# Twenty of the 31 taps of one convolution chunk, on GpSimd in a sum of their own

## The chip, the core and the metric

The kernel runs on one core of a Trainium2 chip. A core has five engines that run their own instruction streams and wait for each other by semaphores: TensorE (PE in the rows, with its weight loads as PEld), VectorE (DVE), ScalarE (ACT), GpSimd (POOL) and SyncE (SP, which here issues the DMAs). The metric is the device time of one launch in microseconds (us); less is better. A row's "ns" is a thousandth of that.

## The reference, cut to what matters

A model block with three token mixers side by side and a mixture of experts is followed by two further layers, on one sequence of 256 tokens with 1024 channels, all in float32. The change lies in the convolution mixer of the first block. It has 256 channels: a gated input `z`, a causal depthwise convolution of width 31 over the tokens, a group norm, and a swish.

```python
def conv_mixer(u, w, b, gn_g, gn_b):
    a, gt = jnp.split(u, 2, axis=-1)
    z = a * jax.nn.sigmoid(gt)
    zp = jnp.pad(z, ((0, 0), (CONV_WIDTH - 1, 0), (0, 0)))
    y = lax.conv_general_dilated(zp, w[:, None, :].astype(dt), (1,), 'VALID', ...,
                                 feature_group_count=CONV_CH) + b
    ...                     # layer norm in groups of 64 channels, then silu
```

```python
mix = jnp.concatenate([o_gla, o_conv, o_diff], axis=-1)
x = x + mix @ w_out[l]
x = x + hier_moe(...)
```

## The kernel before

Channels (or features) lie on the 128 partitions and the 256 tokens along the free dimension, so 256 convolution channels are two chunks of 128 partitions, `a = 0` and `a = 1`. Every large weight matrix arrives by DMA in pieces of 128 x 2048 float32 (`raw`), is rounded by ScalarE into `hi` (L316) and VectorE computes the rest `lo = raw - hi` (L320); TensorE multiplies with both (L340 and L342, or L356 to L358 where the tokens come out on the partitions). So each piece needs ScalarE, then VectorE, then TensorE. The rings of `hi` and `lo` have four buffers each.

`mixer1` (from L744) is the stage of the change, the first 130 us of the run. It projects the input into the three mixers' operands (`psd` buffers of PSUM, two of them in the ring, read out by VectorE or ScalarE before the next projection may write them), then works out the differential attention (`diff1`), the gated linear attention (`gla`) and the convolution; last, ScalarE takes the norms of the three results (`normed`, L822 to L827) and the output projection begins. TensorE also has small products for later (L1113, on DMA'd `araw`) that fill its gaps.

The convolution reads `zp`, the gated input with 30 zero columns ahead; its two chunks are written by L771. Per chunk, VectorE does tap 0 with the bias (L843), then 30 taps, each one `scalar_tensor_tensor` on 128 x 256 (L845): `y = zp[:, a, w:w+256] * cw[w] + y`. The chunk's group mean is a matmul on TensorE (L847), VectorE subtracts it (L848) and ScalarE squares the result (L849). `cw` holds the tap weights and is there from the start.

What sets the order: the code is handed to a list scheduler, which writes one fixed order per engine; engines then run it strictly in that order. The convolution comes late in the code, so its taps are spread over VectorE's row as filler wherever the scheduler saw room, from 31.5 us to 117 us. Each engine stops at an instruction whose semaphore isn't reached, and all that stands behind it on that engine stops too. GpSimd has no work in this stage.

Of the kernel before, what the change touches and what calls it, by code (L numbers as in the profile page):

```python
# [16 lines left out]
OP = mybir.AluOpType  # L17
# [3 lines left out]
P = 128  # L21
# [203 lines left out]
class Net:  # L225
# [514 lines left out]
    def mixer1(self, hl, T):  # L740
        nc = self.nc
# [4 lines left out]
        zp = T([P, 2, 30 + S], "zp")  # L746
# [91 lines left out]
        cw = T([P, 62], "cw")  # L838
        nc.vector.tensor_scalar(cw, self.v("conv_w", 0, 62), 0.5, None, OP.mult)
        cy, sc = T([P, 2, 256], "cy"), self.w512()  # L840
        for a in range(2):
            y = cy[:, a, :]
            nc.vector.tensor_scalar(y, zp[:, a, 0:256], cw[:, 31 * a:31 * a + 1], self.v("conv_b", a), OP.mult, OP.add)  # L843
            for w in range(1, 31):
                nc.vector.scalar_tensor_tensor(y, zp[:, a, w:w + 256], cw[:, 31 * a + w:31 * a + w + 1], y, OP.mult, OP.add)  # L845
            pm = self.ps("a")
            nc.tensor.matmul(pm[:, 0:256], self.k["blk"], y, start=True, stop=True)  # L847
            nc.vector.scalar_tensor_tensor(y, pm[:, 0:256], -1.0 / 64, y, OP.mult, OP.add)  # L848
            nc.scalar.activation(sc[:, 256 * a:256 * a + 256], y, AF.Square)  # L849
# [1217 lines left out]
```

## Time and profile before

| | |
|---|---|
| median of three runs | 1417.76 us (1417.69 to 1421.76) |
| the profiled execution | 1419.36 us |
| its span (first to last instruction) | 1417.6 us |
| TensorE busy | 1365.7 us (96%) |
| VectorE busy | 1056.5 us (75%) |
| ScalarE busy | 771.6 us (54%) |
| GpSimd busy | 0.2 us |
| granted TensorE clock, mean | 0.989 of full |

Busy times are of instructions, which on one engine overlap a little: a row's duration includes the end of an instruction, under which the next one has begun. From start to start, two neighbours on VectorE are some 0.08 us closer than the duration says. The profiled execution lies 1.76 us above its span and 1.60 us above the median of the runs.

### The profile page before, as it was taken

The page shows a single profiled execution, that of the slowest core. Times are in us where ns is not written, and L with a number is a line of the kernel's source. Part 1 is how long each engine was busy: PE and PEld are TensorE (multiplying, and loading weights), DVE is VectorE, ACT ScalarE, POOL GpSimd, SP SyncE. Part 2 cuts the span into 40 slices and gives each one's busy share as a digit, 9 for nine tenths or more (in the row PEclk, how much of TensorE's full clock was granted, in tenths as well). Part 3 has the DMA queues.
Part 4 walks back from the last instruction along what each step waited for, and adds up shares of the span by engine and source line. Part 5 has one row for each costly group of instructions (what it writes and reads, how often), then busy time and mean ns, then how long its engine had stood idle before and what let it go on. Part 6 is the DMA issues. An engine that isn't in the chain of part 4 may idle for free.

```text
span 1417.6 us, 21913 instructions
## 1 busy us (share of the span) xinstructions
PE 1365.7 (96%) x8070; PEld 1093.5 (77%) x8075; DVE 1056.5 (75%) x2424; ACT 771.6 (54%) x1486; POOL 0.2 (0%) x4
## 2 busy tenths in 40 slices
PE   7998899999999999898999999999999999999997
PEld 6756575546888888666888888888888667888886
DVE  8997646537998567766998877998587586877664
ACT  7556433325665554544755556556555554766563
POOL 0000000000000000000000000000000000000000
PEclk9999899999999999999999999999999999999999
DMA  8744568886886458622687675886487632455452
GB/s 311 285 164 161 240 264 324 338 335 240 370 310 249 166 179 305 267 94 86 238 306 294 208 261 193 331 317 230 164 306 283 233 110 99 161 198 196 143 183 71
DMA packets 51391, 326.49 MB, mean 230 GB/s; under 512 B 6209, under 2 KB 7378, under 8 KB 18898
## 3 DMA queue, kind: packets, MB, share of 16 engines
q1 hardware_dynamic: 50994, 324.86, 62.3%
q8 instruction: 64, 1.05, 0.3%
q14 instruction: 45, 0.37, 0.1%
q10 hardware_dynamic: 288, 0.20, 0.1%
HBM read 324.00 MB, written 1.05 MB: 229 GB/s over the span
## 4 chain that ended last, share of the span: by engine, by line
PE 89%; DVE 5%; ACT 3%; DMA 2%; issue 1%; SPq 0%; DVEq 0%; ACTq 0%
PE psd L340 13%; PE pse L340 12%; PE psa L340 11%; PE psd L342 7%; PE pse L342 6%; PE psa L342 6%; PE psd L356 3%; PE psd L358 3%; PE psd L357 3%; PE psd L1849 3%; PE psm L1113 2%; PE pse L1849 2%; PE psa L1905 1%; PE psd L641 1%; PE pse L1526 1%
## 5 line engine op out<-in xcount | busy, mean ns | idle before, releaser
L320 DVE TENSOR_TENSOR lo<-raw,hi 128x512 fp32r<-128x512 f32 x836 | 505.2, 627 | 166.8 <-ACT hi L316 166.3
L316 ACT ACTIVATE hi<-raw 128x1024 fp32r<-128x1024 f32 (+3 forms) x420 | 402.7, 962 | 332.3 <-PE pse L340 79.2
L340 PE MATMUL psd<-hl,hi 128*128 128x512 f32 x592 | 214.3, 403 | 9.1 <-DVE hl L681 6.7
L342 PE MATMUL psd<-hl,lo 128*128 128x256 f32 x640 | 180.5, 284 | 0.0
L340 PE MATMUL pse<-hl,hi 128*128 128x512 f32 x496 | 176.2, 397 | 0.0
L340 PE MATMUL psa<-hl,hi 128*128 128x512 f32 x464 | 164.6, 396 | 0.8 <-ACT hi L316 0.6
L342 PE MATMUL psa<-hl,lo 128*128 128x256 f32 x512 | 143.7, 281 | 0.0
L342 PE MATMUL pse<-hl,lo 128*128 128x256 f32 x512 | 143.3, 280 | 0.0
L340 PEld LDWEIGHTS psd<-hl,hi 128*128 128x128 f32 x592 | 112.0, 190 | 38.5 <-ACT hi L316 8.5
L342 PEld LDWEIGHTS psd<-hl,lo 128*128 128x128 f32 x640 | 122.1, 191 | 1.7 <-DVE lo L320 1.0
L340 PEld LDWEIGHTS pse<-hl,hi 128*128 128x128 f32 x496 | 93.2, 188 | 23.7 <-issue 2.3
L340 PEld LDWEIGHTS psa<-hl,hi 128*128 128x128 f32 x464 | 87.1, 188 | 21.2 <-ACT hi L316 0.9
L342 PEld LDWEIGHTS psa<-hl,lo 128*128 128x128 f32 x512 | 96.7, 189 | 1.7 <-issue 1.0
L342 PEld LDWEIGHTS pse<-hl,lo 128*128 128x128 f32 x512 | 96.6, 189 | 0.2
L1143 DVE SCALAR_TENSOR_TENSOR acc<-araw,cact,acc 128x512 f32<-128x512 f32 x118 | 85.0, 743 | 0.8 <-DMA araw<-wada 0.8
L356 PE MATMUL psd<-hi,hl 128*128 128x512 f32 (+3 forms) x224 | 84.6, 378 | 0.8 <-ACT hl L378 0.4
L357 PE MATMUL psd<-lo,hl 128*128 128x512 f32 (+3 forms) x224 | 83.8, 374 | 0.0
L358 PE MATMUL psd<-hi,hl 128*128 128x512 f32 (+3 forms) x224 | 83.2, 374 | 0.0
L340 PE MATMUL pse<-hT,hi 128*128 128x512 f32 x220 | 77.3, 394 | 0.0
L340 PE MATMUL psd<-hT,hi 128*128 128x512 f32 x220 | 77.2, 394 | 0.0
L342 PE MATMUL pse<-hT,lo 128*128 128x256 f32 x264 | 74.1, 281 | 0.0
L342 PE MATMUL psd<-hT,lo 128*128 128x256 f32 x264 | 74.0, 280 | 0.0
(576 smaller groups left out, 2433.8 us busy)
## 6 DMA issues: line engine op xcount, KB each, us to landing
raw<-w SPq DMA_DIRECT2D x87, 1024.0 KB, 5.0
araw<-wada SPq DMA_DIRECT2D x64, 1024.0 KB, 6.9
raw<-w SPq DMA_DIRECT2D x64, 704.0 KB, 4.1
raw<-egu SPq DMA_DIRECT2D x32, 1024.0 KB, 7.2
raw<-edn SPq DMA_DIRECT2D x16, 1024.0 KB, 6.6
raw<-w2n SPq DMA_DIRECT2D x12, 1024.0 KB, 6.6
raw<-cw SPq DMA_DIRECT2D x8, 1024.0 KB, 6.3
araw<-wadb SPq DMA_DIRECT2D x8, 1024.0 KB, 5.8
```

The source lines that it names most:

```text
L316: nc.scalar.activation(hi[:, f:g], src[:, f:g], AF.Copy)
L320: ins = nc.vector.tensor_tensor(lo[:, f:g], src[:, f:g], hi[:, f:g].bitcast(F32), OP.subtract)
L340: nc.tensor.matmul(ps[:M, :].rearrange("p (a b) -> p a b", a=2), hi[:, o:o + M], xhl[:, k0 + k, :, :], start=st, stop=False)
L342: nc.tensor.matmul(ps[:M, 0:256], lo[:, o:o + M], xhl[:, k0 + k, 0, :], start=False, stop=sp)
L356: nc.tensor.matmul(o, xh, wh, start=st, stop=False)
L357: nc.tensor.matmul(o, xh, wl, start=False, stop=False)
L358: nc.tensor.matmul(o, xl, wh, start=False, stop=sp)
L641: nc.tensor.matmul(ps[:, 0:258], raw[:, o:o + P], self.xg[:, k, :], start=(k == 0), stop=(k == NC - 1))
L1113: self.together(4, lambda j: self.nc.tensor.matmul(self.ada_acc[32 * j:32 * j + 32, :n], lhsT, rhs[:, n * j:n * j + n], start=start, stop= ...
L1143: nc.vector.scalar_tensor_tensor(acc[:, w], raw[:, w], self.cact[:, c, 0:1], acc[:, w], OP.mult, OP.add)
L1526: self.halves(lambda g: nc.tensor.matmul(po[t][64 * g:64 * g + 64, 256 * rp:256 * rp + 256], vn[:, kt, P * (1 + b) + 64 * g:P * (1 + b) + ...
L1849: self.net.halves(lambda h: nc.tensor.matmul(out[p(h)], lhsT[:, p(h)], rhs(h), start=start, stop=stop, tile_position=(0, 64 * h)))
```

## The change

For chunk `a = 0`, taps 1 to 10 stay on VectorE and taps 11 to 30 go to GpSimd, which adds them up in a tile of its own, `cyp`. Tap 11 is one `tensor_scalar` there; each of the 19 others is two instructions: a `tensor_scalar` into `ctp` (one buffer) and a `tensor_tensor` that adds it to `cyp`. At the end VectorE adds `cyp` to its own sum (L857 of the changed kernel). Chunk `a = 1` keeps all its taps on VectorE. Lines after L845 move down by up to 12: VectorE's taps are L848 now, and the subtraction of the mean is L860.

```diff
         for a in range(2):
             y = cy[:, a, :]
             nc.vector.tensor_scalar(y, zp[:, a, 0:256], cw[:, 31 * a:31 * a + 1], self.v("conv_b", a), OP.mult, OP.add)
+
             for w in range(1, 31):
-                nc.vector.scalar_tensor_tensor(y, zp[:, a, w:w + 256], cw[:, 31 * a + w:31 * a + w + 1], y, OP.mult, OP.add)
+                z, c = zp[:, a, w:w + 256], cw[:, 31 * a + w:31 * a + w + 1]
+                if a or w < 11:
+                    nc.vector.scalar_tensor_tensor(y, z, c, y, OP.mult, OP.add)
+                elif w == 11:
+                    yp = T([P, 256], "cyp")
+                    nc.gpsimd.tensor_scalar(yp, z, c, None, OP.mult)
+                else:
+                    tp = T([P, 256], "ctp")
+                    nc.gpsimd.tensor_scalar(tp, z, c, None, OP.mult)
+                    nc.gpsimd.tensor_tensor(yp, yp, tp, OP.add)
+            if a == 0:
+                nc.vector.tensor_tensor(y, y, yp, OP.add)
```

GpSimd's row of the changed kernel, from the end of its start-up; 39 instructions in all, each of which waits for the one ahead of it, since `ctp` and `cyp` pass between them. The first waits for `zp` (L771), the ISA row ahead of it for nothing.

```order
L2074 UNCONDITIONAL_BRANCH
L851 ISA
L851 TENSOR_SCALAR cyp_1148<-zp_202,cw_1133 128x256
L854 TENSOR_SCALAR ctp_1150<-zp_202,cw_1133 128x256
L855 TENSOR_TENSOR cyp_1148<-cyp_1148,ctp_1150 128x256
L854 TENSOR_SCALAR ctp_1153<-zp_202,cw_1133 128x256
L855 TENSOR_TENSOR cyp_1148<-cyp_1148,ctp_1153 128x256
```

Before, that row went from its start-up straight to the branch of the expert stage.

VectorE, in the projections of the differential attention: `lo` is half a weight piece, L810 and L812 read the two `psd` buffers of one projection out. Before:

```order
L320 TENSOR_TENSOR lo_679<-raw_676,hi_678 128x512 x2
L845 SCALAR_TENSOR_TENSOR cy_1135<-zp_202,cw_1133,cy_1135 128x256 x2
L810 TENSOR_REDUCE dss_554<-w_103_630 128x8
L812 TENSOR_SCALAR dqk_629<-psd_555,r_22_198 128x512
L810 TENSOR_REDUCE dss_554<-w_104_634 128x8
```

and now:

```order
L320 TENSOR_TENSOR lo_679<-raw_676,hi_678 128x512 x2
L857 TENSOR_TENSOR cy_1135<-cy_1135,cyp_1148 128x256
L848 SCALAR_TENSOR_TENSOR cy_1135<-zp_202,cw_1133,cy_1135 128x256
L810 TENSOR_REDUCE dss_554<-w_103_630 128x8
L812 TENSOR_SCALAR dqk_629<-psd_555,r_22_198 128x512
```

VectorE's row is the same ahead of this place. One tap has given way to the sum with GpSimd's result, and that row waits for GpSimd's last instruction.

VectorE at the end of the stage, where L1017 (now L1029) reads the last attention product out, L848 (now L860) is the convolution's mean, and `lo` belongs to the output projection. Before:

```order
L1017 TENSOR_SCALAR dqk_861<-pse_1005,subg_857 128x256
L848 SCALAR_TENSOR_TENSOR cy_1135<-psa_1168,cy_1135 128x256
L845 SCALAR_TENSOR_TENSOR cy_1135<-zp_202,cw_1133,cy_1135 128x256
L1157 TENSOR_TENSOR mod_365<-psm_1297,vec 128x16
L845 SCALAR_TENSOR_TENSOR cy_1135<-zp_202,cw_1133,cy_1135 128x256
L1161 SCALAR_TENSOR_TENSOR gs_367<-mod_365,vec 128x8
L320 TENSOR_TENSOR lo_1340<-raw_1337,hi_1339 128x512
L845 SCALAR_TENSOR_TENSOR cy_1135<-zp_202,cw_1133,cy_1135 128x256
L320 TENSOR_TENSOR lo_1345<-raw_1337,hi_1344 128x512 x2
L848 SCALAR_TENSOR_TENSOR cy_1135<-psa_1203,cy_1135 128x256
```

and now:

```order
L1173 SCALAR_TENSOR_TENSOR gs_367<-mod_365,vec 128x8
L1029 TENSOR_SCALAR dqk_861<-pse_1005,subg_857 128x256
L860 SCALAR_TENSOR_TENSOR cy_1135<-psa_1208,cy_1135 128x256
L860 SCALAR_TENSOR_TENSOR cy_1135<-psa_1243,cy_1135 128x256
L827 TENSOR_TENSOR go_1113<-go_1113,w_259_1250 128x512
```

Three taps and three `lo` have left the stretch between the two rows of the mean; the taps are done earlier in VectorE's row, and the `lo` of the output projection too, five of them in the places of taps that GpSimd has taken and three a little later. From the output projection on, all engines' rows are as before.

## Rows read from the trace of the kernel before

**Rows 1.** The page: busy us, share of the span and instructions of each engine.

```profile
PE 1365.7 (96%) x8070; PEld 1093.5 (77%) x8075; DVE 1056.5 (75%) x2424; ACT 771.6 (54%) x1486; POOL 0.2 (0%) x4
```

**Rows 2.** Stretches of `mixer1`: its length, busy us (and instructions) of each engine.

```profile
core 0: us, PE busy (x) PEld busy (x) DVE busy (x) ACT busy (x) POOL busy (x), PEclk, DMA share, GB/s
24.30:51.85 27.55, 26.86 (x154) 23.39 (x152) 27.21 (x80) 18.49 (x32) 0.00 (x0) 1.00 0.75 276
51.85:78.90 27.05, 26.73 (x122) 19.60 (x121) 26.63 (x67) 12.39 (x16) 0.00 (x0) 1.00 0.68 264
78.90:114.90 36.00, 33.34 (x204) 19.21 (x201) 32.97 (x85) 18.16 (x60) 0.00 (x0) 1.00 0.48 175
114.90:119.30 4.40, 3.49 (x21) 1.47 (x22) 4.40 (x12) 0.86 (x3) 0.00 (x0) 1.00 0.00 0
```

**Rows 3.** Three of these stretches, line L845 alone: VectorE's taps.

```profile
24.30:51.85 27.55, 6.60 (x15) 1.00 0.75 276
51.85:78.90 27.05, 12.23 (x27) 1.00 0.68 264
78.90:114.90 36.00, 6.45 (x15) 1.00 0.48 175
```

**Rows 4.** VectorE's groups from 24.3 to 51.85 us: busy us, mean ns | idle before.

```profile
L320 DVE TENSOR_TENSOR lo<-raw,hi 128x512 fp32r<-128x512 f32 x22 | 14.5, 684 | 0.1
L845 DVE SCALAR_TENSOR_TENSOR cy<-zp,cw,cy 128x256 f32<-128x256 f32 x15 | 6.6, 478 | 0.0
L752 DVE SCALAR_TENSOR_TENSOR sog<-psd,w 128x256 f32<-128x256 f32 x2 | 0.8, 424 | 0.2 <-ACT w L368 0.2
L752 DVE SCALAR_TENSOR_TENSOR gqk<-psd,w 128x256 f32<-128x256 f32 x2 | 0.8, 422 | 0.1
L760 DVE TENSOR_SCALAR gv<-psd,r 128x272 f32<-128x272 f32 x1 | 0.5, 501 | 0.0
L896 DVE TENSOR_TENSOR gzk<-gqk,gqk 128x256 f32<-128x256 f32 x1 | 0.4, 419 | 0.0
L1088 DVE COPY cact<-cact 128x256 f32<-128x256 f32 x1 | 0.3, 283 | 0.0
```

**Rows 5.** VectorE in order of time: start us, us; `zp`'s first chunk, and 51.85 us.

```profile
23.90 0.41 DVE L771 SCALAR_TENSOR_TENSOR zp<-w,nrs 128x256 f32<-128x256 f32 x1
...
51.85 0.88 DVE L845 SCALAR_TENSOR_TENSOR cy<-zp,cw,cy 128x256 f32<-128x256 f32 x2
52.65 0.68 DVE L810 TENSOR_REDUCE dss<-w 128x8 f32<-128x512 f32 x1
53.24 0.74 DVE L812 TENSOR_SCALAR dqk<-psd,r 128x512 f32<-128x512 f32 x1
```

**Rows 6.** TensorE in order of time, behind those; in brackets the idle time ahead.

```profile
52.75 1.06 PE L1113 MATMUL psm<-araw,cact 128*32 128x512 f32 x8
54.13 0.47 PE L356 MATMUL psd<-hi,hl 128*128 128x512 f32 x1 [0.32 <-DVE dqk L812]
```

**Rows 7.** ScalarE in order of time, at the end of the stage.

```profile
114.04 0.38 ACT L1016 ACTIVATE w<-pse 128x256 f32<-128x256 f32 x1 [0.46 <-PE pse L1015]
115.37 0.42 ACT L849 ACTIVATE w<-cy 128x256 f32<-128x256 f32 x1 [0.94 <-DVE cy L848]
118.86 0.42 ACT L849 ACTIVATE w<-cy 128x256 f32<-128x256 f32 x1 [3.07 <-DVE cy L848]
119.25 0.69 ACT L490 ACTIVATE w<-psa,eps 128x512 f32<-128x512 f32 x1
```

**Rows 8.** Single groups of 0 to 140 us that bound GpSimd's price.

```profile
L2059 POOL MEMSET const-float32-0.0<- 128x1 f32 x1 | 0.1, 100 | 0.2 <-issue 0.2
L433 DVE MEMSET k_ghead<- 32x1 f32 x4 | 0.2, 59 | 0.1
L490 ACT ACTIVATE cy<-cy,vec 128x256 f32<-128x256 f32 x2 | 1.1, 596 | 0.0
L919 DVE COPY_PREDICATED gSA<-k_gmask,psa 128x512 f32<-128x512 uint8 x7 | 6.2, 883 | 0.2 <-PE psa L918 0.2
```

## The prediction, made before the changed kernel had run

> **What bounds the kernel now.** I read the page's first line, then the stretches of the stage, then single rows in order of time where an engine waits. The whole run is TensorE's: 96% busy, with VectorE at 75% and GpSimd at nothing [rows 1]. That makes GpSimd look free and VectorE worth relieving. But a share over 1417.6 us says nothing on 20 taps that lie in the first 120 us, so the stage has to be read in pieces [rows 2].
>
> From 24.3 us, where the first chunk of `zp` is done (23.90 + 0.41, rows 5), to 51.85 us TensorE is busy 26.86 of 27.55 us and VectorE 27.21: both are full, and neither has slack. From 51.85 to 78.9 us the same holds (26.73 and 26.63 of 27.05). From 78.9 to 114.9 us TensorE has 36.00 - 33.34 = 2.66 us of idle time, VectorE 3.03. Then, from 114.9 to 119.3 us, VectorE is busy without a break and ScalarE does 0.86 us of work: this is the tail, in which ScalarE waits 3.07 us for the mean of the second chunk [rows 7] while VectorE does three last taps and three `lo`. VectorE decides there.
>
> One more place is tight: at 51.85 us. VectorE does two taps, then L810 and L812, which read `psd` out; TensorE had filled the time with L1113 and starts its next projection at 54.13 us, after 0.32 us of waiting for L812 [rows 5, 6]. So what delays VectorE's row ahead of that L812 delays TensorE by the same amount but for nothing, and behind it TensorE has 27 us of work with 0.3 us of idle time, in which a delay can't be won back.
>
> **What the change takes away.** Twenty taps leave VectorE. A tap's row says 478 ns [rows 4]; from start to start it is 0.40 us (the two at 51.85 end where L810 starts, 0.80 us later, rows 5). That is 20 x 0.40 = 8.0 us of VectorE's work, and the new sum L857 takes the place of one more of those starts, at the 419 ns of the nearest two-input row (L896, rows 4), less than a tap. But of 8 us only what stood on the path counts, stretch by stretch:
>
> - up to 51.85 us: VectorE's row is the same as before, 15 taps included [rows 3]. Nothing is gained.
> - 51.85 to 78.9 us: 27 taps become 19, and five `lo` of the output projection move in. 8 x 0.40 = 3.2 us go, 5 x 0.60 = 3.0 come. TensorE bounds this stretch. Nothing is gained.
> - 78.9 to 114.9 us: 15 taps and one `lo` become six taps and three `lo`, so 9 x 0.40 - 2 x 0.60 = 2.4 us less. It can shorten the stretch by no more than TensorE's idle 2.66 us. That idle time has other causes too (a late `araw`, hand-overs between engines), so I take 1 us, with 0 and 2.7 as ends.
> - the tail: three taps and three `lo` are gone from between the two rows of the mean, so ScalarE's second L849 follows its first at once. Gain 3.1 us [rows 7].
>
> Together **4.1 us of gain**, between 3.1 and 5.8. What comes next on the path is ScalarE's chain of norms, which starts with L490 at 119.25 us and is unchanged.
>
> **What the change adds: 39 instructions on GpSimd.** The trace of before shows no GpSimd instruction that reads anything, only memsets of one column at 100 ns, where VectorE takes 59 [rows 8]. So the price is bounded by other engines' rows: 283 ns for VectorE's copy of 128 x 256, the cheapest; 596 ns for ScalarE's dearest row of that size; and, far above, 883 ns for L919, the dearest row of VectorE in the stage [rows 4, 8]. The instruction it is nearest to is the one it replaces, a tap at 478 ns, although one tap becomes two instructions; I take 0.475 us. Then GpSimd is busy for 39 x 0.475 = 18.5 us (11.0 to 34.4). Its first instruction waits for `zp` at 24.3 us; alone, it would end at 42.8 us, and L857 needs it at 51.85. Each instruction waits for the one ahead, so the full duration counts, not the pitch; there is room for 27.55/39 = 0.706 us each.
>
> The second question is whether the two engines can read at once. Rows 4 show what VectorE draws: 256 columns with two inputs in SBUF take 419 ns, 256 columns copied with one input 283. So a copy moves through faster than one column at a time, and a two-input row needs two columns read for each one written: nearly all of VectorE's work up to 51.85 us reads SBUF at twice the rate of one stream. Only four L752 and one L760 take their tensor from PSUM for one side, 4 x 0.42 + 0.50 = 2.2 us. GpSimd's 39 instructions want the same memory in the same 27 us. No row has both at work; the cost of that lies between nothing and all of GpSimd's busy time. A middle value would need both engines to slow each other by halves, and nothing shows that; I take the dear end, that one waits while the other reads, since VectorE's rows leave no reading for a third stream, and give the other end its own chance below. Then VectorE stands still for 18.5 - 2.2 = **16.3 us** (8.8 to 32.2), ahead of L812, whoever goes first: either the taps and `lo` up to 51.85 are late one by one, or GpSimd is late and L857 waits.
>
> The Trainium skill, "SBUF — State Buffer", section "Who interferes with whom", has this as a rule against the change: "A DVE instruction with two SBUF inputs contends with a GpSimd instruction that reads SBUF", and the later one of the two blocks in full. No run here shows it yet. The skill's "GPSIMD Engine Reference", section 3.1, gives 4497 ns for a float32 `tensor_tensor` over 2048 columns; as an estimate from that page, 256 columns are 0.56 us, 39 of them 22 us, and by that price the stop would be 20 us.
>
> **The sum.** The span of 1417.6 us becomes 1417.6 + 16.3 - 4.1 = 1429.8 us, the profiled execution 1431.6; against the median, 1.60 us below the profiled one, it is **1430 us**. With the price from 283 to 596 ns (stop 8.8 to 21.0 us) and the gain's ends it goes from 1420.7 to 1435.7.
>
> **Rivals.** *Side by side.* GpSimd's reads cost VectorE nothing, and its sum is there before 51.85 us, which it is up to 0.706 us an instruction. For it: the simplest reading of GpSimd's 0.2 us. Against it: that VectorE is full and reads two streams. Then the gain stands alone: 1417.8 - 4.1 = 1413.7 us, from 1412 to 1414.7; or, where the scheduler's moves eat it, up to 1418. This is the rival on the other side, and it decides at a stop of 4.1 us: below that the change gains.
>
> *The sum comes late.* GpSimd holds nobody up, but is slow by its own chain, beyond 0.706 us each. Then VectorE runs to 51.85 us undisturbed and stands at L857, with a tap, L810 and L812 queued behind it and TensorE behind these. At 883 ns: 24.3 + 34.4 = 58.7, a stop of 6.9 us, net +2.8: 1420.6 us. It turns slower than before at 24.3 + 39 x t = 51.85 + 4.1, t = 0.81 us. For it: GpSimd's one-column rows are 1.7 times VectorE's. From 1418 to 1432.
>
> *Both.* They take turns and an instruction costs GpSimd 0.7 us or more: at 883 ns the stop is 32.2 us, 1417.8 + 32.2 - 4.1 = 1446 us; from 1438 up.
>
> **Chances.** A run of this kernel can tell some 0.3%, that is 4.3 us: faster is below 1413.5, slower above 1422.0. The forecast (turns, 1420.7 to 1435.7) has 0.56: 0.03 of it within 0.3%, 0.53 slower. Side by side has 0.20, half faster than 1413.5 (0.09) and the rest the same (0.11). The late sum has 0.15: 0.08 the same, 0.07 slower. Both together has 0.09, all slower. Sums: faster 0.09, same 0.22, slower 0.69. The range leaves out the best part of side by side and the worst of both: 1415 to 1444 us.
>
> **What the changed kernel's profile would show.** Turns: VectorE's rows between 24 and 65 us (L320, taps) take longer than 684 and 478 ns or have gaps that no other engine's semaphore ends, GpSimd's rows lie between them, and the L812 behind L857 starts some 16 us after 53.24. Late sum: rows of 684 and 478 ns as before and one long wait at L857 for GpSimd. Side by side: neither, with GpSimd done before 51.85. In all cases the second L849 should follow the first within a microsecond, and everything behind the output projection should be shifted as a whole. I would be wrong if VectorE's durations didn't change while GpSimd is at work, or if a stop before 52 us were won back before 79 us, where I see no idle time on TensorE to win it from.

## The result, and the profile after

The changed kernel takes 1439.35 us (median; 1434.59 to 1439.97), the kernel before, run beside it on the same chip, 1418.54: a ratio of 1.013 with a 95% interval of 1.0108 to 1.0151. The change is slower, by 15 to 21 us by this interval (20.8 us between the medians); the forecast was 1430.0 in a range of 1415 to 1444. The profiled execution took 1439.93 us and its span is 1438.1, against 1417.6 before: 20.5 us more, which the following account divides up.

The page, first line (busy us, share, instructions), and the start of its chain of work that ended last:

```profile
PE 1373.1 (95%) x8070; PEld 1097.1 (76%) x8075; DVE 1058.7 (74%) x2405; ACT 772.6 (54%) x1486; POOL 41.1 (3%) x43
...
PE 87%; DVE 4%; ACT 3%; POOL 3%; DMA 1%; issue 1%; SPq 0%; DVEq 0%; ACTq 0%
```

Against [rows 1], VectorE does 19 instructions fewer and yet is busy 2.2 us longer. And GpSimd is 3% of the chain: its 41 us lie on the path that sets the end. That line by itself says that the new engine wasn't used "for free".

By form, from 24 to 70 us, to be read against [rows 4] (busy us, mean ns | idle time before, and what ended it):

```profile
L854 POOL TENSOR_SCALAR ctp<-zp,cw 128x256 f32<-128x256 f32 x19 | 23.8, 1252 | 1.8
L320 DVE TENSOR_TENSOR lo<-raw,hi 128x512 fp32r<-128x512 f32 x22 | 17.6, 828 | 0.1
L855 POOL TENSOR_TENSOR cyp<-cyp,ctp 128x256 f32<-128x256 f32 x19 | 15.7, 824 | 1.6
L848 DVE SCALAR_TENSOR_TENSOR cy<-zp,cw,cy 128x256 f32<-128x256 f32 x16 | 11.0, 722 | 0.0
```

The same 22 `lo` that took 684 ns take 828, and a tap takes 722 instead of 478 ns. No idle time is shown: what VectorE loses is inside its rows' durations, so a list of waits can't show it, only durations compared form by form. (That it is GpSimd which it loses the time to is shown by the experiments, not by these rows.) GpSimd's rows are long too: 1252 and 824 ns. Later, when VectorE stands still, a pair runs undisturbed, and GpSimd's row in order of time gives its price (start us, us):

```profile
63.41 0.92 POOL L854 TENSOR_SCALAR ctp<-zp,cw 128x256 f32<-128x256 f32 x1
64.42 0.72 POOL L855 TENSOR_TENSOR cyp<-cyp,ctp 128x256 f32<-128x256 f32 x1
```

From start to start the product and the sum take 1.83 us, hand-overs of 0.09 to 0.1 us included. So 19 such pairs and the first product are some 36 us undisturbed, where the prediction had 18.5.

What happens at the join (VectorE, then TensorE, in order of time; idle time ahead in brackets; then TensorE before, behind the L356 of [rows 6]):

```profile
59.29 1.48 DVE L320 TENSOR_TENSOR lo<-raw,hi 128x512 fp32r<-128x512 f32 x2
68.83 0.42 DVE L857 TENSOR_TENSOR cy<-cy,cyp 128x256 f32<-128x256 f32 x1 [8.07 <-POOL cyp L855]
69.18 0.48 DVE L848 SCALAR_TENSOR_TENSOR cy<-zp,cw,cy 128x256 f32<-128x256 f32 x1
69.57 0.68 DVE L810 TENSOR_REDUCE dss<-w 128x8 f32<-128x512 f32 x1
70.17 0.74 DVE L812 TENSOR_SCALAR dqk<-psd,r 128x512 f32<-128x512 f32 x1
```

```profile
38.56 0.62 PE L340 MATMUL psd<-hl,hi 128*128 128x512 f32 x1 [2.86 <-DVE gv L760]
...
58.48 1.06 PE L1125 MATMUL psm<-araw,cact 128*32 128x512 f32 x8
71.06 0.76 PE L356 MATMUL psd<-hi,hl 128*128 128x512 f32 x1 [11.52 <-DVE dqk L812]
71.62 0.63 PE L357 MATMUL psd<-lo,hl 128*128 128x512 f32 x1
72.05 0.63 PE L358 MATMUL psd<-hi,hl 128*128 128x512 f32 x1
...
76.29 0.40 PE L356 MATMUL psd<-hi,hl 128*128 128x512 f32 x1
```

```profile
54.44 0.40 PE L357 MATMUL psd<-lo,hl 128*128 128x512 f32 x1
54.67 0.40 PE L358 MATMUL psd<-hi,hl 128*128 128x512 f32 x1
```

Against [rows 5], L812 comes 16.93 us late (53.24 to 70.17), and in two portions. VectorE reaches the join at 60.7 instead of 51.85 us, 8.8 us late, and then waits 8.07 us for GpSimd's last sum. Against [rows 6], TensorE's next projection starts at 71.06 instead of 54.13. It comes back slow: 12 matmuls stand 0.43 us apart where they stood 0.23 us apart, which is 2.4 us more. The stretches show why (length, busy us of PE, PEld, DVE, ACT and POOL, granted clock, DMA share, GB/s):

```profile
24.00:60.70 36.70, 31.73 (x168) 25.51 (x166) 36.56 (x81) 21.07 (x34) 33.62 (x30) 0.95 0.66 233
59.40:68.83 9.43, 0.14 (x4) 0.00 (x0) 1.37 (x2) 0.18 (x1) 8.59 (x10) 0.67 0.60 229
71.00:76.30 5.30, 5.24 (x13) 4.12 (x14) 3.82 (x8) 0.00 (x0) 0.00 (x0) 0.50 0.31 108
```

TensorE did nothing for 11.5 us, the granted clock fell, and the first 5.3 us of work ran at 0.50, the lower of the two levels (1.2 GHz), where [rows 2] have 1.00. The 0.95 of the first row has a pause ahead of it too: TensorE stood for 2.86 us up to 38.56, waiting for VectorE's L760, and ran at 0.50 from 38.7 to 42.1 us. That is not an extra cost at the join: VectorE, late by its own long rows, has 0.14 us of idle time on its way there.

ScalarE at the end of the stage, against [rows 7]:

```profile
134.96 0.72 ACT L861 ACTIVATE w<-cy 128x256 f32<-128x256 f32 x2 [0.94 <-DVE cy L860]
136.76 0.69 ACT L490 ACTIVATE w<-psa,eps 128x512 f32<-128x512 f32 x1 [1.07 <-PE psa L822]
```

The two squares are neighbours now: the wait of 3.07 us is gone. But L490 doesn't follow at once, as it did; it waits 1.07 us for L822 on TensorE, which stands behind a piece of filler, L1125. The first square is at 134.96 instead of 115.37 us (19.6 later), L490 at 136.76 instead of 119.25 (17.5 later): the tail gave 2.1 us.

Up to L490 the account is 16.9 (stop) + 2.4 (half clock) - 1.8 (gain) = 17.5 us. The rest of the 20.5 comes later, where all engines' rows are those of before. Two stretches of TensorE are at a lower granted clock that were at 1.00 in the profile before:

```profile
338.00:343.00 5.00, 5.00 (x17) 1.53 (x18) 0.00 (x0) 1.89 (x3) 0.00 (x0) 0.66 0.56 236
595.00:600.00 5.00, 5.00 (x61) 2.56 (x54) 0.59 (x3) 0.57 (x3) 0.00 (x0) 0.66 0.56 203
```

They cost 1.6 and 1.4 us. Whether they belong to the change stays open. Such stretches come and go between executions (before's profile has one at 646 us that the kernel with the taps out, below, lacks; that one has one at 598), and one of after's four runs had a mean clock of 0.986 instead of 0.981 and a span of 1432.8 us. But the other three lie within 1.2 us of 1438 us, and the two-input kernel below, as late as this one, has such stretches at the same places (339 and 595 us).

### The profile page after: what moved, and what is told of

It reads as the page before. It is cut to its first block, busy times and chain, and to the rows that moved or that the text cites. A ratio compares the mean times of both kernels' runs of the same rounds, so it can differ in the third digit from the quotient of the medians.

```text
span 1438.1 us, 21943 instructions
## 1 busy us (share of the span) xinstructions
PE 1373.1 (95%) x8070; PEld 1097.1 (76%) x8075; DVE 1058.7 (74%) x2405; ACT 772.6 (54%) x1486; POOL 41.1 (3%) x43
## 4 chain that ended last, share of the span: by engine, by line
PE 87%; DVE 4%; ACT 3%; POOL 3%; DMA 1%; issue 1%; SPq 0%; DVEq 0%; ACTq 0%
PE psd L340 12%; PE pse L340 12%; PE psa L340 10%; PE psd L342 7%; PE pse L342 6%; PE psa L342 6%; PE psd L356 3%; PE psd L358 3%; PE psd L357 3%; PE psd L1861 3%; POOL ctp L854 2%; PE pse L1861 2%; PE psm L1125 2%; POOL cyp L855 1%; PE psa L1917 1%
## 5 line engine op out<-in xcount | busy, mean ns | idle before, releaser
L356 PE MATMUL psd<-hi,hl 128*128 128x512 f32 (+3 forms) x224 | 85.9, 384 | 12.8 <-DVE dqk L812 11.5
```

The lines of the kernel that those rows point to most:

```text
L356: nc.tensor.matmul(o, xh, wh, start=st, stop=False)
```

## The experiments

Two theories, after the trace: **turns**, VectorE loses time to each GpSimd instruction, and the late sum is added to that; and its rival, that it is all the **late sum**, VectorE's long rows being only a by-product. Within the turns it was open what makes a turn. The place to read is L812, the row behind the join in after; its distance to the first `zp` (L771), from which both engines start, is 29.34 us before (53.24 - 23.90, rows 5). Last column: by how much the distance grew.

| kernel | median, us | ratio to before, 95% interval | L812 against `zp`, us later |
|---|---|---|---|
| after | 1439.35 | 1.013 (1.0108 to 1.0151) | 16.8 |
| taps out | 1417.17 | 0.9993 (0.9981 to 1.0005) | -0.5 |
| unread sum | 1429.84 | 1.0081 (1.0053 to 1.0109) | 9.2 |
| writes only | 1418.12 | 1.0000 (0.9985 to 1.0015) | 0.1 |
| join late | 1428.36 | 1.0064 (1.0041 to 1.0087) | 8.3 |
| ten taps | 1424.56 | 1.0035 (1.0019 to 1.0051) | 5.4 |
| one input | 1419.71 | 1.0024 (1.0004 to 1.0044) | 2.3 |
| two inputs | 1439.19 | 1.0149 (1.0124 to 1.0175) | 17.0 |
| adds only | 1427.31 | 1.0058 (1.0036 to 1.0081) | 9.3 |
| late, six memsets a tap, two tiles (and one step of `newton` less) | 1417.16 | 0.9991 (0.9978 to 1.0003) | -0.1 |
| late, six memsets a tap, one tile | 1423.46 | 1.0032 (1.0017 to 1.0047) | -0.5 (the sum is awaited behind it) |

### The gain alone: the taps taken out

```diff
-            for w in range(1, 31):
+            for w in range(1, 31 if a else 11):
                 nc.vector.scalar_tensor_tensor(...)
```

> The 20 taps of chunk 0 (11 to 30) are left out of the computation; GpSimd does nothing and nothing is joined. The engines' rows are those of the change without L857. This measures the gain alone. By my sum it is 4.1 us: 1418.5 - 4.1 = 1414.4 us. By the trace of the change, where 19.3 us of delay behind L812 and the slow matmuls had shrunk to 17.5 at the end of the stage, it is 1.8 us: 1416.7. In both cases VectorE's L320 rows stay at 684 ns.

```profile
116.94 0.69 ACT L490 ACTIVATE w<-psa,eps 128x512 f32<-128x512 f32 x1 [1.08 <-PE psa L822]
```

L490 starts at 116.94 us, 2.3 before 119.25, and the median differs from before by nothing that can be measured (the 4.1 us of the forecast would be a ratio of 0.9971, outside the interval). So twenty taps for free are worth about 2 us. TensorE sets the pace where the taps lie, and what VectorE leaves it doesn't take. Here as in after, the scheduler has also put the attention's rows from 78 us to the end of the stage into another order than before; the 2.3 us and after's 1.8 include that.

### The turns alone: a sum that nobody reads

All 60 taps stay on VectorE, the join is left out, GpSimd does its 39 instructions all the same. All rows of the other engines are before's.

```diff
+                nc.vector.scalar_tensor_tensor(y, z, c, y, OP.mult, OP.add)
+                if a == 0 and w == 11:
                     nc.gpsimd.tensor_scalar(yp, z, c, None, OP.mult)
+                elif a == 0 and w > 11:
                     nc.gpsimd.tensor_scalar(tp, z, c, None, OP.mult)
                     nc.gpsimd.tensor_tensor(yp, yp, tp, OP.add)
-            if a == 0:
-                nc.vector.tensor_tensor(y, y, yp, OP.add)
```

> Before, with all 60 taps on VectorE, and GpSimd doing its 39 instructions beside them into a sum that nobody reads. No wait is added anywhere, and the rows of all engines but GpSimd are those of before. Turn-taking: each GpSimd instruction costs VectorE 8.8/39 = 0.23 us, 8.8 us in all, up to 11 as VectorE never idles now: 1427 to 1430 us, L320 rows longer than 684 ns until GpSimd ends. Late sum alone (no turns): 1418.5 us, no difference, and GpSimd's 39 instructions take 0.92 us each as they did while VectorE stood still, 36 us.

By form, 24.3 to 70 us:

```profile
L320 DVE TENSOR_TENSOR lo<-raw,hi 128x512 fp32r<-128x512 f32 x24 | 19.5, 840 | 0.1
L846 DVE SCALAR_TENSOR_TENSOR cy<-zp,cw,cy 128x256 f32<-128x256 f32 x19 | 13.3, 732 | 0.0
```

Nobody waits for GpSimd and the kernel is 11 us slower: the late sum can't be all of it. VectorE's rows are as long as in after.

### Writing without reading

After, with the products and sums of taps 12 to 30 replaced by memsets of the same tiles; the join stays.

```diff
-                    nc.gpsimd.tensor_scalar(tp, z, c, None, OP.mult)
-                    nc.gpsimd.tensor_tensor(yp, yp, tp, OP.add)
+                    nc.gpsimd.memset(tp, 0.0)
+                    nc.gpsimd.memset(yp, 0.0)
```

> The change, with 38 of GpSimd's 39 instructions replaced by memsets of 128 x 256, which read nothing; taps 12 to 30 of chunk 0 are so left out of the computation. If it is GpSimd's reading that costs VectorE time, VectorE's L320 rows stay at 684 ns, GpSimd is done well before 52 us, L857 waits for nothing, and the time is that of the kernel with the taps out, 1414 to 1417 us. If any work on GpSimd costs it (writes too), 38 x 0.1 to 0.2 us come on top: 1418 to 1425 us.

```profile
L320 DVE TENSOR_TENSOR lo<-raw,hi 128x512 fp32r<-128x512 f32 x32 | 20.8, 685 | 0.4 <-ACT hi L316 0.4
L855 POOL MEMSET cyp<- 128x256 f32 x19 | 6.0, 315 | 1.1
L854 POOL MEMSET ctp<- 128x256 f32 x19 | 5.9, 311 | 1.3 <-POOLq L2071 0.3
```

`lo` is back at 685 ns, and the time is that of before (1.0000). The 19 memsets of `ctp` wait for nothing and are over at 7.7 us; the 19 of `cyp` run beside VectorE's work, from 26.5 to 33.6 us, and cost it nothing. So writing alone doesn't cost; something that the products and sums do beyond it does, and they read (that they also compute and last longer, this run doesn't separate). The Trainium skill, "SBUF — State Buffer", section "Who interferes with whom", states this exception too, and here the trace agrees.

### The join moved back

After, with VectorE's sum ordered behind the last tap of the second chunk; the group means get a loop of their own, and no other row of VectorE, ScalarE or GpSimd moves.

```diff
-                    nc.vector.scalar_tensor_tensor(y, z, c, y, OP.mult, OP.add)
+                    ins = nc.vector.scalar_tensor_tensor(y, z, c, y, OP.mult, OP.add)
-            if a == 0:
-                nc.vector.tensor_tensor(y, y, yp, OP.add)
+        self.after(nc.vector.tensor_tensor(cy[:, 0, :], cy[:, 0, :], yp, OP.add), ins)
+        for a in (1, 0):
+            y = cy[:, a, :]
```

> The change with L857 moved behind the last tap of chunk 1, some 60 rows later on VectorE; no other row moves. Turn-taking and late sum both at work: the wait of 8.1 us at the join goes, and with it the idle time after which TensorE ran at half clock (2.4 us); the 8.8 us of turns stay, and the last eight or nine GpSimd instructions, which ran while VectorE waited, now cost it some 2 us more: 1439.4 - 8.1 - 2.4 + 2 = 1431 us. If the waiting were all of it: 1416.7 us. If turns were all of it: 1439 us.

VectorE, then TensorE, in order of time:

```profile
62.57 0.73 DVE L812 TENSOR_SCALAR dqk<-psd,r 128x512 f32<-128x512 f32 x1
```

```profile
63.45 0.47 PE L356 MATMUL psd<-hi,hl 128*128 128x512 f32 x1 [3.04 <-DVE dqk L812]
```

1428.36 us, 2.6 below the sum worked out: without the wait of 8 us at the join, and with TensorE's pause down from 11.52 to 3.04 us (3.4 us at half clock are left behind it, from 64.4 us), 11 us of after's loss are gone, 9 by the ratios; L812 is still 8.3 us late. So moving the join wins back about half of after's loss, the late sum with the half clock that its pause brings, and the turns that are left are the other half. And with the join where nobody waits for it the change is still 0.64% slower than before.

### Ten taps instead of twenty

```diff
-                if a or w < 11:
+                if a or w < 21:
...
-                elif w == 11:
+                elif w == 21:
```

> Ten taps instead of twenty on GpSimd (taps 21 to 30, 19 instructions); VectorE adds the sum 40 rows later in its order, behind the two L812 of the place at 52 us. Theory (VectorE loses some 0.23 us for each GpSimd instruction that reads, and the rest of the loss was the late join): GpSimd ends near 47 us, VectorE doesn't wait for it, L812 starts 19 x 0.23 = 4.4 us later than before's 53.24, near 57.6, and the median is some 3 to 4 us above before, 1422, at most 2 us being won in the tail. Rival (each GpSimd instruction costs 16.9/39 = 0.43 us, the late join being only another form of it): L812 at 61.5, 1425 to 1427. Rival (the loss needs the long chain, ten taps are free): L812 at 53.2 to 54, 1417 to 1419.

1424.56 us, L812 5.4 us later, no wait at the join: between the theory's 4.4 and its rival's 8. So 0.23 us for each reading instruction alike is too little; what follows explains the rest. Nothing is won at the end either, as ScalarE's row there shows:

```profile
121.16 0.42 ACT L861 ACTIVATE w<-cy 128x256 f32<-128x256 f32 x1 [0.94 <-DVE cy L860]
124.65 0.42 ACT L861 ACTIVATE w<-cy 128x256 f32<-128x256 f32 x1 [3.07 <-DVE cy L860]
```

Taps of the second chunk fill the tail here, and its wait is before's 3.07 us.

### What makes a turn: one input, two inputs, adds only

The unread sum three times more, with other instructions on GpSimd: 39 `tensor_scalar` with one tensor input; one of these and 38 `tensor_tensor` with two; one and 19 sums without the products.

```diff
-                    nc.gpsimd.tensor_tensor(yp, yp, tp, OP.add)
+                    nc.gpsimd.tensor_scalar(yp, tp, c, None, OP.mult)          # one input
```

> The kernel before, all taps on VectorE, plus 39 GpSimd instructions that nobody reads, all of them tensor_scalar with one tensor input (the add of each tap is replaced by a second tensor_scalar on ctp). Theory (VectorE loses 10.3/39 = 0.26 us per GpSimd instruction that reads, whatever it reads): L812 near 63.5 as with the adds, 1428 to 1430. Rival (the loss goes by what GpSimd reads: 39 input tensors here, 58 with the adds): 53.24 + 10.3 x 39/58 = 60.2, 1425 to 1427. Rival (only GpSimd's two-input instructions cost VectorE anything): L812 at 53.2, 1418.

```diff
-                    nc.gpsimd.tensor_scalar(tp, z, c, None, OP.mult)
+                    nc.gpsimd.tensor_tensor(tp, z, zp[:, a, 0:256], OP.mult)   # two inputs
```

> The kernel before, all taps on VectorE, plus 39 GpSimd instructions that nobody reads, all but the first of them tensor_tensor with two tensor inputs (the product of each tap is zp times zp instead of zp times a weight). Theory (0.26 us per GpSimd instruction that reads): L812 near 63.5, 1428 to 1430, although GpSimd is done sooner. Rival (by what GpSimd reads, 77 tensors instead of 58): 53.24 + 10.3 x 77/58 = 66.9, 1431 to 1433. Rival (by GpSimd's busy time, 0.72 us instead of 0.82 on the mean): 53.24 + 10.3 x 0.72/0.82 = 62.3.

```diff
-                    nc.gpsimd.tensor_scalar(tp, z, c, None, OP.mult)
-                    nc.gpsimd.tensor_tensor(yp, yp, tp, OP.add)
+                    nc.gpsimd.tensor_tensor(yp, yp, z, OP.add)                 # adds only
```

> The kernel before, all taps on VectorE, plus GpSimd instructions that nobody reads: one tensor_scalar and then only the 19 adds, cyp = cyp + zp, with no products between them. Theory (an instruction of GpSimd with two tensor inputs costs VectorE some 0.45 us, as the 38 of the two-input run did with 16.9 us, one with one input some 0.1 us): 19 x 0.45 = 8.5 us, L812 some 8.5 us later against zp than before, 1426 to 1428, although only half as many instructions are there as with the products. Rival (0.26 us per GpSimd instruction that reads, whatever it reads): 20 x 0.26 = 5.2 us, 1422 to 1424.

One input, by form from 24 to 75 us, and one stretch in order of time:

```profile
L853 POOL TENSOR_SCALAR cyp<-ctp,cw 128x256 f32<-128x256 f32 x17 | 24.7, 1453 | 1.6
L320 DVE TENSOR_TENSOR lo<-raw,hi 128x512 fp32r<-128x512 f32 x32 | 20.9, 685 | 0.4 <-ACT hi L316 0.4
L846 DVE SCALAR_TENSOR_TENSOR cy<-zp,cw,cy 128x256 f32<-128x256 f32 x31 | 16.1, 555 | 0.0
```

```profile
36.38 3.69 DVE L320 TENSOR_TENSOR lo<-raw,hi 128x512 fp32r<-128x512 f32 x6
39.98 1.01 DVE L846 SCALAR_TENSOR_TENSOR cy<-zp,cw,cy 128x256 f32<-128x256 f32 x2
36.84 4.33 POOL L853 TENSOR_SCALAR cyp<-ctp,cw 128x256 f32<-128x256 f32 x1
```

This is the surprise. VectorE's `lo` keeps its 685 ns, six in a row go through in 3.69 us, and the GpSimd instruction beside them takes 4.33 us instead of 0.93. VectorE has no gap behind them either: GpSimd ends 1.1 us after the last `lo`, beside two taps, which take 1.01 us together instead of 0.88 [rows 5]. Row by row against before, 12 of VectorE's rows ahead of L812 are longer, by 0.13 to 0.23 us each: six taps and six others, but no `lo` of 512 columns. Together that is 2.2 us, all of the delay. So with one input GpSimd gives way most of the time and now and then takes a short turn; 20 of its instructions before L812 cost 2.3 us, some 0.1 us each.

Two inputs, from 24 to 70 us, then adds only, from 24 to 46 us, where GpSimd is at work:

```profile
L320 DVE TENSOR_TENSOR lo<-raw,hi 128x512 fp32r<-128x512 f32 x22 | 19.9, 935 | 0.0
L853 POOL TENSOR_TENSOR cyp<-cyp,ctp 128x256 f32<-128x256 f32 x19 | 17.4, 918 | 1.5
L852 POOL TENSOR_TENSOR ctp<-zp 128x256 f32<-128x256 f32 x19 | 16.8, 883 | 1.4
```

```profile
L851 POOL TENSOR_TENSOR cyp<-cyp,zp 128x256 f32<-128x256 f32 x19 | 16.5, 867 | 1.5
L320 DVE TENSOR_TENSOR lo<-raw,hi 128x512 fp32r<-128x512 f32 x10 | 8.6, 879 | 0.0
```

Thirty-eight two-input instructions delay L812 by 17.0 us, 0.45 us each; nineteen by 9.3 us, 0.49 each (of which 1.2 us are a wait of `lo` for ScalarE's `hi` at 49.8 us, when GpSimd was done; TensorE had stood for 5.83 us up to 43.9, waiting for VectorE). The median of the two-input run is 20.4 us above before's, more than the 17.0 at L812: TensorE waits for VectorE more often there, and it runs at half clock from 69.2 to 76.0 us, around such waits, which L812 doesn't see. Against that my rate of 0.26 us an instruction "whatever it reads" would have given 10 and 5 us: it falls, and so do the rivals that go by tensors read (13.7 us for two inputs) or by busy time (9). After's loss is put together from these prices: ahead of the join GpSimd did 14 sums and 16 products, 14 x 0.45 + 16 x 0.1 = 7.9 us of the 8.8 measured; ten taps, 9 x 0.45 + 10 x 0.1 = 5.1 of 5.4. What VectorE waits out can be seen on its smallest rows in after (VectorE, then GpSimd, in order of time; last, such a row of VectorE before):

```profile
29.57 0.68 DVE L320 TENSOR_TENSOR lo<-raw,hi 128x512 fp32r<-128x512 f32 x1
30.17 0.70 DVE L1089 TENSOR_TENSOR rr<-rr,rw 128x16 f32<-128x16 f32 x1
```

```profile
29.90 0.94 POOL L855 TENSOR_TENSOR cyp<-cyp,ctp 128x256 f32<-128x256 f32 x1
30.93 0.93 POOL L854 TENSOR_SCALAR ctp<-zp,cw 128x256 f32<-128x256 f32 x1
```

```profile
29.25 0.16 DVE L1077 TENSOR_TENSOR rr<-rr,rw 128x16 f32<-128x16 f32 x1
```

GpSimd's sum comes 0.35 us before `lo` ends and takes 0.94 instead of 0.72 us; VectorE's row of 16 columns, elsewhere 0.16 us, takes 0.70 and ends with GpSimd's sum (30.87 and 30.84). So VectorE's small row waits out the rest of the sum, and the sum has waited for a part of `lo`. The next product of GpSimd runs its undisturbed 0.93 us beside rows of VectorE of which one, with 16 columns, is longer (0.30 instead of 0.16 us).

The rule that the prediction drew on ("SBUF — State Buffer", same section) makes no difference between one and two inputs on GpSimd's side. For two the traces agree with it; for one only in part: there the wait is GpSimd's, nearly all of it, through `lo` rows that began after it did.

### A late sum without readers

Six memsets for each of the taps 12 to 30, first on both tiles in turn, then all on `cyp`, one behind another. The first form's kernel differs in one more place, `newton`, which the second form has as it was.

```diff
-                    nc.gpsimd.tensor_scalar(tp, z, c, None, OP.mult)
-                    nc.gpsimd.tensor_tensor(yp, yp, tp, OP.add)
+                    for _ in range(3):                     # second form: range(6), yp alone
+                        nc.gpsimd.memset(tp, 0.0)
+                        nc.gpsimd.memset(yp, 0.0)
...
-        for _ in range(4):                     # newton, first form alone
+        for _ in range(3):
```

> As the changed kernel, but each of the taps 12 to 30 on GpSimd is six memsets (114 in all, these taps are left out of the result); the sum is still awaited at the same row of VectorE. A late sum without readers. Theory: VectorE's rows keep 684 and 478 ns and it stands at the join until GpSimd is done, near 68 us; the stop of some 15 to 17 us is paid in full, TensorE starts again at half clock after its idle time (12 matmuls at a pitch of 0.43 instead of 0.23 us), and the median is 1434 to 1437, as if the taps were computed there. Rival (the changed kernel's time beyond 16.9 - 1.8 us comes from VectorE and GpSimd being at work together, not from TensorE's pause): no half-clock stretch, 1431 to 1433.

The first form missed its purpose: the memsets of `ctp` wait for nothing and were done before `zp` came, and GpSimd was finished at 47.4 us. Its 1417.16 us is the time of the taps out, but not a clean second run of it: a step of `newton` is missing, three instructions of VectorE, and from 77 us on the rows of TensorE, VectorE and ScalarE stand in another order.

> A late sum without readers, second form: the changed kernel with each of the taps 12 to 30 on GpSimd replaced by six memsets of cyp behind one another (114 in all; these taps are left out of the result). At the 0.378 us from start to start that memsets had there, they end at 25.8 + 114 x 0.378 = 68.9 us, and the sum is awaited at the same row of VectorE. Theory (a stop is paid in full whatever makes it, and TensorE's pause behind it brings half clock): VectorE's rows at 684 and 478 ns, a wait of some 16 us at the join, L812 near 70, the next 12 matmuls at a pitch of 0.43 instead of 0.23 us, and 1434 to 1437, as in the changed kernel. Rival (the half clock there comes from the two engines being at work together): no stretch at half clock behind the wait, 1431 to 1433.

The memsets end at 68.2 us, near the 68.9 worked out, but the order places the sum 20 rows later on VectorE, behind the two L812 of 52.4 us and ahead of the next pair; I had taken it to be the same row. So the wait is 6.5 us and not 16, and the time of 1434 to 1437 was not to be had. In order of time, VectorE, then TensorE:

```profile
68.22 0.42 DVE L856 TENSOR_TENSOR cy<-cy,cyp 128x256 f32<-128x256 f32 x1 [6.47 <-POOL cyp L854]
```

```profile
72.56 0.77 PE L356 MATMUL psd<-hi,hl 128*128 128x512 f32 x1 [6.39 <-DVE dqk L812]
73.12 0.63 PE L357 MATMUL psd<-lo,hl 128*128 128x512 f32 x1
```

and ScalarE at the end of the stage:

```profile
124.99 0.69 ACT L490 ACTIVATE w<-psa,eps 128x512 f32<-128x512 f32 x1 [1.08 <-PE psa L822]
```

The point in question is answered all the same. VectorE's wait of 6.47 us is handed to TensorE in full (6.39), and its matmuls come back 0.43 us apart, until 78.2 us, with no reader on GpSimd anywhere near: the half clock follows the pause, not the two engines' work together. Against the taps out, L490 is 8.1 us later (124.99 to 116.94), more than the pause by itself; 6.0 of them are left at the end of the two profiled executions, whose later stretches at half clock differ.

## Why the prediction was right, and where it was not

The direction was right, and 1439.35 us lies in the range, 9 us above the forecast. Its working was right in part, and two of its errors cancelled.

- **What bounds the kernel**: held. TensorE's share and VectorE's say nothing on these taps; the place at 52 us does. TensorE waited 11.52 us there for L812 and won nothing back before 79 us.
- **The gain, 4.1 us**: mis-sized; 1.8 in after, 2.3 with the taps out. The 3.07 us at ScalarE did vanish, but 1.07 of it came back as a wait for L822 behind a piece of TensorE's filler. The prediction said what comes next on the path, "ScalarE's chain of norms", and missed that L490 has a second input, TensorE's norm sums. The 1 us taken out of TensorE's idle time before 114.9 us didn't come: the first square is even 0.3 us later than stop and half clock explain.
- **The price of a GpSimd instruction, 0.475 us**: wrong, by nearly two. It was taken from the VectorE tap as the "nearest" row. Undisturbed it is 0.92 and 0.72 us and 0.1 for each hand-over. The upper end of the bounds, 883 ns, from a row that had nothing to do with GpSimd, was near the truth (1.83 us / 2 = 0.915). The break-even of *the sum comes late*, 0.81 us, was exceeded.
- **The turns**: the step "VectorE stands still for all of GpSimd's busy time" failed. The traces show the middle value that the prediction set aside: of 39 instructions, half (the products) cost VectorE about 0.1 us and the other half 0.45, in sum 8.8 us ahead of the join and not 16.3. GpSimd pays its own part, 44.3 us for what would take 36 undisturbed.
- **The stop, 16.3 us**: it measured 16.9, and this is luck in the sum: a price of half the size times turns of twice the size. What set the stop's length is GpSimd's own end, 24.5 + 44.3 = 68.8 us: with the join where it is, VectorE would have stood there until then without any turns of its own, so its 8.8 us and the wait of 8.1 follow each other but are not two causes that add up. Undisturbed, GpSimd would have been done near 24.5 + 36 = 60.5 us, as an estimate from its undisturbed rows; the late sum alone would then have made a stop of some 8.6 us, and that GpSimd was held up by VectorE the rest. In kind it was the rival *both*, VectorE slowed and then waiting for the late sum, which had 0.09 and was priced at 1446 us because it kept the full turns. The check that was named for the forecast, "L812 some 16 us after 53.24", couldn't tell the two apart; the other one, a long wait at L857, did.
- **Not in the sum at all**: the half clock behind TensorE's pause, 2.4 us, and the two stretches at the lower level far behind, 3.0 us, whose cause is open. Forecast net 16.3 - 4.1 = 12.2; measured 16.9 - 1.8 + 2.4 + 3.0 = 20.5 us.
- **Side by side**, the rival on the other side: excluded by the unread sum, 1.0081 (1.0053 to 1.0109), and by the two-input run, 1.0149 (1.0124 to 1.0175), for GpSimd work in which two-input instructions take part. For work with one input it is nearly true (1.0024, 1.0004 to 1.0044).

Can a version pay? By these prices not with these instructions; only twenty and ten taps were run. A tap that goes to GpSimd saves VectorE 0.40 us and costs it 0.45 + 0.1 us of turns, so by this working any number of taps loses where both engines are full, and the ceiling with all twenty taps gone is 2 us, less than a measurement can tell. What stays open is why the short turns of one-input work fell on VectorE's taps and small rows and never on a `lo` of 512 columns.

## What to carry to other kernels

Before moving work to an idle engine, take the work out and look at the ceiling: here it was 2 us of 8 us of VectorE's time, since VectorE was busy but TensorE set the pace. Then count what the new engine's instructions read at the same time as the busy one: GpSimd instructions with two tensor inputs cost a VectorE that is full of two-input work some 60% of their own length (0.45 of 0.72 us), memsets cost nothing. And where the result comes back, look at what is queued behind the join on that engine, and at how long TensorE pauses for it: part of the pause is paid a second time in clock.

## What the runs showed of the hardware that was not expected

- GpSimd's `tensor_scalar` on 128 x 256 float32 with a weight per partition takes 0.92 us undisturbed, longer than its two-input `tensor_tensor`, 0.72; a memset of that size 0.31. VectorE does product and sum in one instruction in 0.48.
- Beside a full VectorE, one-input GpSimd instructions gave way (4.33 us for one beside six `lo` of unchanged length), while two-input ones took 0.45 us each from VectorE.
- After pauses of 6.4 and 11.5 us TensorE's next matmuls of 512 columns were 0.43 us apart, not 0.23, for 12 or more of them (granted clock 0.50). Pauses of 2.9 to 6.0 us that VectorE's slow rows made were followed by half clock as well, 3.4 to 6.8 us of it.
